# Five instead of two pairs of AC heads divided ahead of their flips, two heads on GpSimd, with all causal additions there

## The chip, the cores and the metric

One core of a Trainium2 chip runs the whole program in one launch. The metric is device time in microseconds (us), lower is better; of several runs the median counts. The profile is that of one execution.

## What is computed

Two layers of a decoder trunk on 256 tokens of width 1024, in float32. Each layer is half a SwiGLU feed-forward step, a mixer with three groups of heads, and a second half step:

```
h = h + 0.5 * swiglu(rms_norm(h, g1), w_gate1, w_up1, w_down1)
u = rms_norm(h, mix_norm);  P = u @ w_in
A: 4 query heads, one key/value head, keys chosen per query by an indexer (top 64)
B: 4 heads, plain causal attention (there is one block of 256 keys only)
C: 8 "forget" heads: s = q.k * scale + c[q] - c[k], c = cumsum(log_sigmoid(f + bias)),
   causal softmax, times v, times sigmoid(gate)
h = h + concat(o_A, o_B, o_C) @ w_out
h = h + 0.5 * swiglu(rms_norm(h, g2), w_gate2, w_up2, w_down2)
```

## The kernel before, in words

Every weight is split by ScalarE (L126, "high") and VectorE (L130, "low") into two float32r parts, and each product of the large matrices is three TensorE passes (`mm3`, L342). Weights come in by SyncE's DMA queue (L100) into five raw buffers; `Weights.pump`, `high` and `low` say where in the program order a unit is split. The schedule is manual: each engine runs its instructions in the order in which the program emits them, and waits where data or a buffer is not ready. TensorE's order, too, is the order of emission.

In a layer's mixer the loop at L1229 runs over the column chunks of `w_in` in 32 numbered steps (12 matmuls each for the chunks here); work on the side is hung on a step by `at_step(n, fn)` and run by `run_side`. Among it are the log gates and their running sums (`cumsum`, `sums_out`, `sums_in`, L902 to L922): a scan on VectorE, a write of the sums to DRAM, and three DMAs that read them back spread over all partitions into `first` (128 keys, all 8 heads; it takes over the buffer `tab`) and `later` (two tiles of 4 heads, `laterkT` and `laterlater`). The causal mask is added to the spread sums by `causal_part(i)` (L930): parts 0 and 1 on GpSimd at step 28, parts 2 and 3 on VectorE where the order below says `w2` and `w3`.

At step 30 the string EARLY is run, and after step 32 the string AC_ORDER. Each word is one piece of work, the letter what, the number a head or a pair of heads: `s` scores of a pair, `m` mask and row maximum of a head (L1092, VectorE), `e` its exponentials (L1102, ScalarE), `n` reciprocals of a pair's row sums (L1108), `d` a division of a head's probabilities (L1120; two instructions, of 128 and of 256 columns), `F`/`f` flips of a pair (24 TensorE transposes for its two heads, L180), `y` copies of the flipped pair out of PSUM (L193, one half of each bank on VectorE and ScalarE), `v` values, `o` the pair's output with its split (L1157), `h`/`r` parts of the output projection, `j`, `q`, `p` splits of weights. A- and C-heads are numbered 0 to 11, pairs 0 to 5; pairs 0 and 1 are the A-heads, 2 to 5 the forget heads.

Pairs in `divided` (0 and 1) have their probabilities divided before the flip. The others instead spread their reciprocals to 128x256 (`roots`, L1112), have that turned by four more transposes in the flip (L1131, `ident,tmp` in the profile), copied out with it (512 columns instead of 384), and for forget heads multiplied by the gate on GpSimd (L1144) before the output is multiplied by the result (L1165). `outT` then casts the output on ScalarE (L1172), and for forget heads takes the low part on GpSimd (L1180):

```
A.copy(hh, o)
oT[k] = (hh, hl)
high[p] = hl, o, hh, G if kind == "C" else V
if emit is None:
    low(p)
```

The B-heads run through the same functions at earlier steps, with the flip, the copies and the values in `both_scores` (L1204, the word `S`); their copies are all on ScalarE.

Of the kernel before, what the change touches and what calls it, by code (L numbers as in the profile page):

```python
# [10 lines left out]
F32 = mybir.dt.float32  # L11
# [3 lines left out]
ALU = mybir.AluOpType  # L15
# [3 lines left out]
P = 128  # L19
S = 256  # L20
D = 1024
# [5 lines left out]
TOPK = 64  # L27
# [10 lines left out]
WARM = 6  # L38
BRIDGE = 3
P_BUFS = 4  # L40
EARLY = "S Q q m0 e0 m1 e1 m2 e2 b0 b1 m3 j B0 B1 e3"
AC_ORDER = """
    h0 n0 d0 C n1 d1 d2 d3 T c0 F0 k0 F1 y0 y1 c1 k1 s2 v0 v1 m4 m5 g o0 o1 e4 e5 s3 s4
    h1 m6 m7 w2 e6 e7 l q q n2 n3 w3 m8 m9 h2 h3
    F2 f3 y2 y3 s5 v2 v3 e8 e9 m10 m11 e10 e11 o2 o3 n4 j
    r0 r1 n5 j F4 F5 y4 y5 h4 j v4 v5 o4 o5 j
    p h5 h6 h7 Z r2 N p r3 p r4 p M x2 p x3 p
"""
B_TURN, A_ROPE, B_STEP, A_ROOT, A_TURN, SUMS_STEP, TOP_STEP, A_STEP = 18, 18, 20, 21.3, 28.5, 21, 15, 30


CHUNKS = [
# [102 lines left out]
def kernel(ctx: ExitStack, tc: tile.TileContext, x, ffn1_norm, ffn1_w_gate, ffn1_w_up, ffn1_w_down,  # L155
# [10 lines left out]
    at = ctx.enter_context(tc.tile_pool(name="at", bufs=1))  # L166
# [5 lines left out]
    V, A, G, T = nc.vector, nc.scalar, nc.gpsimd, nc.tensor  # L172

    def bank(tag):
        return psum.tile([P, 512], F32, name="ps_" + tag, tag=tag)
# [6 lines left out]
    def turned(ps, dst, copies):  # L182
        for e, copy in enumerate(copies):
            d = dst[..., 64 * e:64 * e + 64]
            n = 64
            for k in d.shape[1:-1]:
                n *= k
            src = ps[e][:, :n]
            if len(d.shape) == 3:
                src = src.rearrange("p (b j) -> p b j", j=64)  # L190
            else:
                src = src.rearrange("p (a b j) -> p a b j", a=d.shape[1], j=64)
            copy(d, src)  # L193
# [4 lines left out]
    def tmp(n):  # L198
        return tp.tile([P, 512], F32, name="tmp", tag="tmp")[:, :n]
# [39 lines left out]
    W = Weights(tc, raw_pool, split_pool)  # L239
# [89 lines left out]
    causal = cp.tile([P, 3 * P], F32, name="causal")  # L329
# [12 lines left out]
    def mm3(o, lhs, rhs, start, stop):  # L342
        mm(o, lhs[0], rhs[0], start, False)
        mm(o, lhs[0], rhs[1], False, False)
        mm(o, lhs[1], rhs[0], False, stop)
# [344 lines left out]
    def mixer(l, norm, nxt):  # L690
        side, count = [], itertools.count()
        step = [0]

        def at_step(n, fn):
            side.append((n, next(count), fn))

        def run_side():
            due = sorted(x for x in side if x[0] <= step[0])
            for x in due:
                x[2]()  # L700
            side[:] = [x for x in side if x[0] > step[0]]
# [47 lines left out]
        st = {}  # L749
# [44 lines left out]
        def post_ib(ps):  # L794
# [10 lines left out]
            for t in range(2):  # L805
                x = small[t][:, None, 0:64]
# [24 lines left out]
                A.activation(la, la, AF.Ln, bias=1.0)  # L831
                A.activation(small[0][:, 0:1], ones[:, 0:1], AF.Exp)

            at_step(SUMS_STEP - 3, log_sigmoid)
            def forget():
                V.scalar_tensor_tensor(lf, fg, 0.0, la, op0=ALU.min, op1=ALU.subtract)

            at_step(SUMS_STEP - 2, forget)
            st["ikT"] = at.tile([P, 1, S], F32, name="ikT", tag="qs")

            def turn_ik():
# [42 lines left out]
                V.match_replace(out=st["score"][t], in_to_replace=m8, in_values=st["score"][t], imm_value=-3e38)  # L884

            def amask_begin():
                st["amask"] = at.tile([P, 3 * P], F32, name="amask", tag="amask")
                G.tensor_copy(st["amask"][:TOPK, 0:P], causal[:TOPK, 0:P])

            at_step(A_STEP - 4, amask_begin)  # L890

            def amask():
                am, score = st["amask"], st["score"]
                for d, x in ((am[:, P:], score[1]), (am[TOPK:, :P], score[0][TOPK:])):
                    V.tensor_scalar(d, x, -2e38, NEG, op0=ALU.is_gt, op1=ALU.mult)

            at_step(A_STEP - 0.5, amask)

            for r in range(TOPK // 8):
                at_step(TOP_STEP + 2 * r, lambda: topk(1))  # L900
# [20 lines left out]
                    nc.sync.dma_start(to, bass.AP(tensor=src.tensor, offset=src.offset + h * S,  # L921
                                                    ap=[[0, P], [S, k], [1, n]]))  # L922

            at_step(SUMS_STEP + 1, cumsum)
            at_step(SUMS_STEP + 3, sums_out)
            at_step(SUMS_STEP + 5, sums_in)
            for i in range(2):
                at_step(A_STEP - 2, lambda i=i: causal_part(i))

        def causal_part(i):  # L930
            x = st["first"][:, 2 * i:2 * i + 4] if i % 2 == 0 else st["later"][i // 2][:, :, 1]
            (V if i > 1 else G).tensor_tensor(x, x, causal[:, None, 0:P].to_broadcast([P, 4, P]), op=ALU.add)

        def post_a(ps):
            ss = sm.tile([P, 2, 5], F32, name="ssa", tag="ss")
# [40 lines left out]
        def post_b(ps):  # L976
# [34 lines left out]
            def qk_b(kind, h):  # L1011
                return st["bT"][:, h // 2 * 2], st["bT"][:, h // 2 * 2 + 1]

            st["B"] = run_heads([("B", h) for h in range(4)], qk_b, lambda i, fn: at_step(B_STEP + i, fn))

        c_ss = at.tile([P, 2, 2, 8], F32, name="c_ss", tag="c_ss")
# [35 lines left out]
        def tanh():  # L1052
            ps, hr = st.pop("cg"), st["hr"]
            sg = at.tile([P, 2, 512], F32, name="sg", tag="sg")
            for t in range(2):
                A.activation(sg[:, t], ps[t], AF.Tanh, scale=hr[:, t:t + 1])
            st["sg"] = sg
            for _ in range(2):
                bank("gu")


        def run_heads(hs, qk, emit=None):
            pj, pt, op, sums, bs, wide, flipped, gated, high = {}, {}, {}, {}, {}, {}, {}, {}, {}
            divided = range(2)
            blocks = ((slice(0, P), slice(0, P), slice(0, P)), (slice(P, 3 * P), slice(P, S), slice(0, S)))
            tag = "acc" if emit else "gu"

# [65 lines left out]
            def spread(p):  # L1133
                both = pp.tile([P, 8, P], F32, name="pT", tag="pT", bufs=2)
                kind, h = hs[2 * p]
                turned(flipped.pop(p), both[:, :6] if p in divided else both,
                       (A.copy if emit else V.tensor_copy, A.copy))
                pt[p] = [both[:, 3 * e:3 * e + 3].rearrange("p a b -> p (a b)") for e in range(2)]
                gated[p] = both[:, 6:8].rearrange("p a b -> p (a b)")
                if kind == "C":  # L1140
                    o = st["gate"][:, h // 2]
                    if p not in divided:
                        o = tmp(S)
                        G.tensor_tensor(o, gated[p], st["gate"][:, h // 2], op=ALU.mult)  # L1144
                    gated[p] = o
# [36 lines left out]
            if emit is None:  # L1182
                return scores, masks, exps, roots, divide, flip, spread, values, outT
# [10 lines left out]

        hs = [("A", h) for h in range(4)] + [("C", h) for h in range(8)]
        scores, masks, exps, roots, divide, flip, spread, values, outT = run_heads(hs, qk_ac)

        def c_T(ps, src, g, at):
# [5 lines left out]
        def both_scores(_):  # L1204
# [8 lines left out]
            for p in range(2):  # L1213
                b_values(p, st["keys"][p][:, S:])

        todo = dict(S=both_scores, D=divide, d=lambda i: divide(i, V), s=scores, m=masks, e=exps, n=roots, F=flip, y=spread, v=values, o=outT,
                    Q=lambda _: W.high(), q=lambda _: W.high(), j=lambda _: W.low(),
                    b=lambda p: st["B"][1](p), B=lambda p: st["B"][2](p), T=lambda _: tanh(), w=causal_part)

        def do(text):  # L1220
            for word in text.split():
                todo[word[0]](int(word[1:] or 0))

        at_step(A_STEP, lambda: do(EARLY))

        oT = {}
        posts = dict(ib=post_ib, a=post_a, b=post_b, ck=post_ck, cq=post_cq, cv=post_cv, cg=post_cg)
        index_queries()
        for name, cols in CHUNKS[1:]:  # L1229
            n = sum(c[1] for c in cols)  # L1230
            ps = [bank("gu") for _ in range(2)]
            for u in range(4):
                w = W.take()
                for kk in range(2):
                    k = 2 * u + kk
                    for t in range(2):
                        ts = slice(t * P, (t + 1) * P)
                        mm3(ps[t][:, :n], (norm.h[:, k, ts], norm.l[:, k, ts]), [v[:, kk] for v in w],
                            k == 0, k == KT - 1)
                step[0] += 1  # L1240
                run_side()
                if step[0] < A_STEP and step[0] != 8:
                    W.pump()
            posts[name](ps)
            if step[0] == 8:
                W.pump(2)
# [70 lines left out]
        def norm_out(_):  # L1317
# [5 lines left out]
            for t in range(2):  # L1323
# [3 lines left out]
                    p=lambda _: W.pump(), Z=residuals, N=norm_T, M=norm_out)  # L1327
# [23 lines left out]
    for l in range(DEPTH):  # L1351
        norm = ffn(norm, lambda: Norm(1, l), lambda: before_mixer(l), l == 0)
        norm = mixer(l, norm, lambda: Norm(2, l))
        norm = ffn(norm, (lambda: Norm(0, l + 1)) if l + 1 < DEPTH else None)
# [37 lines left out]
```

## Time and profile before

| | |
|---|---|
| median of 3 runs | 1001.65 us (1001.61 to 1001.83) |
| profiled execution, its own time | 1001.55 us |
| span of the profile, first to last instruction | 999.8 us |
| granted TensorE clock, mean | 0.999 |
| busy: PE, DVE, ACT, POOL | 995.5, 799.3, 597.4, 162.0 us |

Times in the timelines are microseconds from the start of the span. PE is TensorE's matmuls, PEld its weight loads, DVE VectorE, ACT ScalarE, POOL GpSimd, SPq SyncE's queue. The first layer's flips of forget heads lie between 294 and 302 us, the second layer's 494.9 us later, with the same instructions.

### The profile page before, as it was taken

What the parts mean: (1) busy time and instruction counts of PE and PEld (TensorE: products, weight loads), DVE (VectorE), ACT (ScalarE), POOL (GpSimd) and SP (SyncE); (2) the same over time, 40 slices, a digit from 0 to 9 for tenths busy, and PEclk for the clock granted to TensorE, in tenths of its full rate; (3) what the DMA queues carried; (4) which work ended last, traced back from release to release, by engine and by line L of the source; (5) the groups of instructions that cost most, each with busy time, mean ns of one, the idle gap of its engine ahead of it and who ended that gap; (6) DMA issues with size and microseconds to landing.
All of it is one profiled execution on the core that took longest, in us unless ns stands there. A gap on an engine that the chain in (4) does not pass through costs nothing.

```text
span 999.8 us, 15219 instructions
## 1 busy us (share of the span) xinstructions
PE 995.5 (100%) x5692; PEld 856.5 (86%) x5692; DVE 799.3 (80%) x1482; ACT 597.4 (60%) x1118; POOL 162.0 (16%) x188
## 2 busy tenths in 40 slices
PE   9999999999999999999999999999999999999998
PEld 8888888888878888888888888889888788888887
DVE  5978778789998777777888777787899977777775
ACT  6655555597786555555465555556968765555552
POOL 2003000058812000000000020001677210000000
PEclk9999999999999999999999999999999999999999
DMA  9865647475725555555655655565566164464731
GB/s 291 274 224 160 224 156 238 129 238 188 230 87 169 173 164 193 187 195 196 199 169 176 207 183 198 185 208 166 192 211 232 58 208 159 140 238 148 232 128 43
DMA packets 133498, 184.80 MB, mean 185 GB/s; under 512 B 7152, under 2 KB 106800, under 8 KB 133424
## 3 DMA queue, kind: packets, MB, share of 16 engines
q1 hardware_dynamic: 133392, 183.82, 56.2%
q8 instruction: 45, 0.74, 0.3%
q14 instruction: 29, 0.24, 0.1%
q10 hardware_dynamic: 32, 0.01, 0.0%
HBM read 182.75 MB, written 1.06 MB: 184 GB/s over the span
## 4 chain that ended last, share of the span: by engine, by line
PE 98%; DMA 1%; SPq 0%; ACT 0%; issue 0%; DVE 0%
PE ps_gu L340 66%; PE ps_acc L340 30%; PE ps_acc L180 1%; DMA raw<-in_ffn_w_up_dram 1%; PE ps_acc L375 1%; PE ps_gu L180 1%; SPq L100 0%; SPq L225 0%; PE ps_gu L375 0%; PE ps_acc L970 0%; ACT wh L126 0%; PE ps_acc L402 0%; PE ps_acc L844 0%; PE ps_acc L905 0%; DVE trunk L419 0%
## 5 line engine op out<-in xcount | busy, mean ns | idle before, releaser
L130 DVE TENSOR_TENSOR wl<-raw,wh 128x1024 fp32r<-128x1024 f32 (+2 forms) x342 | 421.6, 1240 | 27.1 <-ACT wh L126 27.1
L126 ACT CAST wh<-raw 128x1024 fp32r<-128x1024 f32 (+2 forms) x341 | 341.2, 1037 | 14.4 <-PE ps_acc L340 7.7
L340 PE MATMUL ps_gu<-xhl,wh 128*128 128x512 f32 (+1 forms) x1472 | 347.6, 388 | 0.2 <-ACT wh L126 0.2
L340 PEld LDWEIGHTS ps_gu<-xhl,wh 128*128 128x128 f32 x1472 | 272.5, 188 | 54.4 <-ACT wh L126 0.7
L340 PEld LDWEIGHTS ps_gu<-xhl,wl 128*128 128x128 f32 x1472 | 187.5, 191 | 4.1 <-DVE wl L521 0.2
L340 PE MATMUL ps_gu<-xhl,wl 128*128 128x256 f32 (+1 forms) x1472 | 190.3, 282 | 0.0
L484 DVE TENSOR_TENSOR tmp<-ps_gu,tmp 128x256 f32<-128x256 f32 x176 | 72.8, 422 | 109.3 <-ACT tmp L483 109.0
L340 PE MATMUL ps_acc<-wh,hh 128*128 128x512 f32 (+1 forms) x352 | 137.3, 390 | 0.0
L340 PE MATMUL ps_acc<-wl,hh 128*128 128x512 f32 (+1 forms) x352 | 137.0, 389 | 0.0
L340 PE MATMUL ps_acc<-wh,hl 128*128 128x512 f32 (+1 forms) x352 | 136.6, 388 | 0.0
L340 PE MATMUL ps_gu<-wh,xhl 128*128 128x512 f32 (+2 forms) x448 | 133.4, 375 | 0.0
L483 ACT COPY tmp<-ps_gu 128x256 f32<-128x256 f32 x176 | 63.4, 371 | 92.1 <-PE ps_gu L340 91.9
L498 ACT CAST hh<-tmp 128x256 fp32r<-128x256 f32 x80 | 32.6, 407 | 120.2 <-DVE tmp L495 120.2
L340 PEld LDWEIGHTS ps_gu<-wh,xhl 128*128 128x128 f32 x448 | 82.5, 188 | 14.1 <-issue 1.7
L490 ACT ACTIVATE tmp<-tmp 128x256 f32<-128x256 f32 x88 | 36.9, 419 | 82.7 <-DVE tmp L488 82.5
L340 PE MATMUL ps_gu<-wl,xhl 128*128 128x512 f32 (+2 forms) x224 | 83.2, 372 | 0.0
L351 POOL TENSOR_TENSOR y_n<-msq,minus_half 128x2 f32<-128x2 f32 x6 | 7.0, 1174 | 441.9 <-DVE msq L350 441.9
L340 PEld LDWEIGHTS ps_acc<-wh,hl 128*128 128x128 f32 x352 | 66.1, 188 | 13.9
L340 PEld LDWEIGHTS ps_acc<-wh,hh 128*128 128x128 f32 x352 | 66.2, 188 | 12.6
L340 PEld LDWEIGHTS ps_acc<-wl,hh 128*128 128x128 f32 x352 | 66.3, 188 | 12.3 <-DVE wl L130 0.2
L340 PEld LDWEIGHTS ps_gu<-wl,xhl 128*128 128x128 f32 x224 | 42.2, 188 | 5.9
L508 DVE TENSOR_TENSOR tmp<-tmp,rb 128x256 f32<-128x256 f32 x88 | 37.7, 428 | 3.0
(237 smaller groups left out, 901.5 us busy)
## 6 DMA issues: line engine op xcount, KB each, us to landing
raw<-in_ffn_w_down_dram SPq DMA_DIRECT2D x44, 1024.0 KB, 5.0
raw<-in_ffn_w_gate_dram SPq DMA_DIRECT2D x42, 1024.0 KB, 6.9
raw<-in_ffn_w_up_dram SPq DMA_DIRECT2D x42, 1024.0 KB, 7.8
raw<-in_w_in_dram SPq DMA_DIRECT2D x24, 1024.0 KB, 5.1
raw<-in_w_out_dram SPq DMA_DIRECT2D x8, 1024.0 KB, 5.0
raw<-in_w_in_dram SPq DMA_DIRECT2D x4, 768.0 KB, 5.0
raw<-in_w_in_dram SPq DMA_DIRECT2D x4, 656.0 KB, 4.2
raw<-in_ffn_w_gate_dram SPq DMA_DIRECT2D x3, 512.0 KB, 7.5
```

Of the source, the lines that this page charges most:

```text
L126: self.nc.scalar.copy(hv, src)
L130: (engine or self.nc.vector).tensor_tensor(lv, self.srcs[self.n_low], hv.bitcast(F32), op=ALU.subtract)
L180: T.transpose(b[:, 64 * i:64 * i + 64], src[r], ident[r, r])
L340: T.matmul(o, l, r, start=start, stop=stop, skip_group_check=True)
L351: G.tensor_tensor(y, dst, minus_half[:, :n], op=ALU.pow)
L375: T.transpose(ps[:, i, t * P:(t + 1) * P], trunk[:, t, (2 * mp + i) * P:(2 * mp + i + 1) * P], ident)
L483: A.copy(o, ps[:, 1])
L484: V.tensor_tensor(o, ps[:, 0], o, op=ALU.add)
L490: A.activation(th, t_, AF.Tanh, scale=0.5)
L498: (V.tensor_copy if late else A.copy)(hh, t_)
L508: V.tensor_tensor(t_, t_, norm.rb, op=ALU.mult)
```

## The change

It puts pairs 2, 3 and 4 into `divided`. Their heads are divided by VectorE (5, 6, 7, 9) and by GpSimd (4 and 8, the new word `G`). It moves the running sums (`cumsum` from step 22 to 26, `sums_out` from 24 to 27, `sums_in` from 26 to 28), the turn of the A-heads (28.5 to 26), the building of the A-mask and causal parts 0 and 1 (from steps 28 and 30 to the word `a` in EARLY), and one weight split (from step 29 to the word `j` in EARLY). Causal parts 2 and 3 go to GpSimd at the word `W`; all parts read a copy of the mask that VectorE (at `a`) and ScalarE (at `W`) write just before. One half of the B-heads' copies goes from ScalarE to VectorE.

```diff
-EARLY = "S Q q m0 e0 m1 e1 m2 e2 b0 b1 m3 j B0 B1 e3"
+EARLY = "S j a Q q m0 e0 m1 e1 m2 e2 b0 b1 m3 j B0 B1 e3"
 AC_ORDER = """
-    h0 n0 d0 C n1 d1 d2 d3 T c0 F0 k0 F1 y0 y1 c1 k1 s2 v0 v1 m4 m5 g o0 o1 e4 e5 s3 s4
-    h1 m6 m7 w2 e6 e7 l q q n2 n3 w3 m8 m9 h2 h3
-    F2 f3 y2 y3 s5 v2 v3 e8 e9 m10 m11 e10 e11 o2 o3 n4 j
-    r0 r1 n5 j F4 F5 y4 y5 h4 j v4 v5 o4 o5 j
+    h0 n0 d0 C n1 d1 d2 d3 T c0 F0 k0 F1 y0 y1 c1 k1 W s2 v0 v1 m4 m5 g o0 o1 e4 e5 s3 s4
+    h1 m6 m7 n2 G4 d5 e6 e7 l q q n3 d6 d7 m8 m9 h2 h3
+    F2 f3 y2 y3 s5 v2 v3 e8 e9 m10 m11 e10 e11 o2 n4 G8 d9 o3 j n5
+    r0 r1 j F4 F5 y4 y5 j h4 v4 v5 o4 o5 j
     p h5 h6 h7 Z r2 N p r3 p r4 p M x2 p x3 p
 """
-B_TURN, A_ROPE, B_STEP, A_ROOT, A_TURN, SUMS_STEP, TOP_STEP, A_STEP = 18, 18, 20, 21.3, 28.5, 21, 15, 30
+B_TURN, A_ROPE, B_STEP, A_ROOT, A_TURN, SUMS_STEP, TOP_STEP, A_STEP = 18, 18, 20, 21.3, 26, 26, 15, 30
...
-                st["amask"] = at.tile([P, 3 * P], F32, name="amask", tag="amask")
+                st["amask"] = at.tile([P, 4 * P], F32, name="amask", tag="amask")
...
-                for d, x in ((am[:, P:], score[1]), (am[TOPK:, :P], score[0][TOPK:])):
+                for d, x in ((am[:, P:3 * P], score[1]), (am[TOPK:, :P], score[0][TOPK:])):
                     V.tensor_scalar(d, x, -2e38, NEG, op0=ALU.is_gt, op1=ALU.mult)
-
-            at_step(A_STEP - 0.5, amask)
+                V.tensor_copy(am[:, 3 * P:], causal[:, 0:P])
+                for i in range(2):
+                    causal_part(i)
+
+            st["mask"] = amask
...
-            at_step(SUMS_STEP + 1, cumsum)
-            at_step(SUMS_STEP + 3, sums_out)
-            at_step(SUMS_STEP + 5, sums_in)
-            for i in range(2):
-                at_step(A_STEP - 2, lambda i=i: causal_part(i))
+            at_step(SUMS_STEP, cumsum)
+            at_step(SUMS_STEP + 1, sums_out)
+            at_step(SUMS_STEP + 2, sums_in)
...
-            (V if i > 1 else G).tensor_tensor(x, x, causal[:, None, 0:P].to_broadcast([P, 4, P]), op=ALU.add)
+            mask = st["amask"][:, None, 3 * P:].to_broadcast([P, 4, P])
+            G.tensor_tensor(x, x, mask, op=ALU.add)
+
+        def late_causal(_):
+            A.copy(st["amask"][:, 3 * P:], causal[:, 0:P])
+            for i in range(2, 4):
+                causal_part(i)
...
-            divided = range(2)
+            divided = range(5)
...
-                       (A.copy if emit else V.tensor_copy, A.copy))
+                       (V.tensor_copy, A.copy))
...
+G=lambda i: divide(i, G), W=late_causal, a=lambda _: st["mask"]()
...
-                if step[0] < A_STEP and step[0] != 8:
+                if step[0] < A_STEP - 1 and step[0] != 8:
                     W.pump()
+                if step[0] == A_STEP - 1:
+                    W.high()
```

The log gates stay at steps 18 and 19, written as plain numbers now.

## Rows read from the trace of the kernel before

**Rows 1.** The page, part 1: busy time, share of the span and instructions of each engine.

```profile
PE 995.5 (100%) x5692; PEld 856.5 (86%) x5692; DVE 799.3 (80%) x1482; ACT 597.4 (60%) x1118; POOL 162.0 (16%) x188
```

**Rows 2.** The page, part 4: the chain that ended last, shares by engine.

```profile
PE 98%; DMA 1%; SPq 0%; ACT 0%; issue 0%; DVE 0%
```

**Rows 3.** Waits of TensorE's weight loads, whole span: us in total, times, longest.

```profile
PEld ps_gu L340 <- issue: 3.7, 12, 0.4
...
PEld ps_acc L180 <- ACT pT L193: 0.4, 2, 0.2
```

**Rows 4.** Timeline, TensorE, layer 1: start, length, engine, line, tiles, count.

```profile
294.55 0.59 PE L180 MATMUL ps_gu<-ident,p 64*128 64x64 f32 x12
294.97 0.29 PE L180 MATMUL ps_gu<-ident,tmp 64*128 64x64 f32 x4
295.09 0.54 PE L180 MATMUL ps_acc<-ident,p 64*128 64x64 f32 x12
...
300.79 0.59 PE L180 MATMUL ps_gu<-ident,p 64*128 64x64 f32 x12
```

**Rows 5.** Timeline, ScalarE, layer 1: first exponential of head 8, cast of the outputs.

```profile
296.36 0.40 ACT L1102 ACTIVATE p<-tmp,nm 128x128 f32<-128x128 f32 x1
...
299.88 0.70 ACT L1172 CAST oh<-tmp 128x256 fp32r<-128x256 f32 x2
```

**Rows 6.** Timeline, ScalarE, layer 1: two copies of 384 and two of 512 columns.

```profile
285.32 0.86 ACT L193 COPY pT<-ps_gu 128x384 f32<-128x384 f32 x2
...
301.63 1.09 ACT L193 COPY pT<-ps_gu 128x512 f32<-128x512 f32 x2 [1.04 <-PE ps_gu L180]
```

**Rows 7.** Timeline, GpSimd, layer 1: gate products of pairs 2, 3, low parts.

```profile
296.12 1.42 POOL L1144 TENSOR_TENSOR tmp<-pT,cT 128x256 f32<-128x256 f32 x2 [20.03 <-ACT pT L193]
300.35 2.44 POOL L1180 TENSOR_TENSOR ol<-tmp,oh 128x256 fp32r<-128x256 f32 x2 [2.82 <-ACT oh L1172]
```

**Rows 8.** Timeline, VectorE, layer 1, around the flips of forget heads.

```profile
286.98 0.29 DVE L1092 CUSTOM_DVE_ANT_0 tmp<-ps_gu,tab 128x128 f32<-128x128 f32 x1
...
290.80 0.69 DVE L932 TENSOR_TENSOR tab<-tab,causal 128x512 f32<-128x512 f32 x1
...
295.29 0.69 DVE L193 COPY pT<-ps_gu 128x512 f32<-128x512 f32 x1 [0.67 <-PE ps_gu L180]
...
298.79 1.22 DVE L130 TENSOR_TENSOR wl<-raw,wh 128x1024 fp32r<-128x1024 f32 x1
...
300.43 1.75 DVE L130 TENSOR_TENSOR wl<-raw,wh 128x1024 fp32r<-128x1024 f32 x1
```

**Rows 9.** Timeline, GpSimd, layer 1: the division of one B-head.

```profile
263.51 0.60 POOL L1120 TENSOR_SCALAR p<-p,sums 128x128 f32<-128x128 f32 x1
...
264.09 0.92 POOL L1120 TENSOR_SCALAR p<-p,sums 128x256 f32<-128x256 f32 x1
```

**Rows 10.** Timeline, VectorE, layer 1: the divisions of heads 1 to 3.

```profile
283.53 1.44 DVE L1120 TENSOR_SCALAR p<-p,sums 128x128 f32<-128x128 f32 x6
```

**Rows 11.** Timeline, GpSimd and VectorE, layer 1: causal parts and the low beside them.

```profile
273.58 1.26 POOL L932 TENSOR_TENSOR tab<-tab,causal 128x512 f32<-128x512 f32 x1
274.81 1.27 POOL L932 TENSOR_TENSOR laterkT<-laterkT,causal 128x512 f32<-128x512 f32 x1
...
273.85 3.32 DVE L130 TENSOR_TENSOR wl<-raw,wh 128x1024 fp32r<-128x1024 f32 x1
```

**Rows 12.** Groups by line, whole span, VectorE: count, busy us, mean ns, idle before.

```profile
L1112 DVE COPY tmp<-sums 128x256 f32<-128x256 f32 x8 | 2.3, 294 | 0.3
```

**Rows 13.** Timeline, SyncE's queue, layer 1: issues of the sums and the weights.

```profile
258.83 0.41 SPq L911 DMA_DIRECT2D sums_of<-tmp  x1
...
263.60 0.37 SPq L921 DMA_DIRECT2D tab<-sums_of  x1
...
268.53 0.38 SPq L100 DMA_DIRECT2D raw<-in_ffn_w_gate_dram  x1
```

**Rows 14.** DMA issues, stretch 258 to 283 us: count, KB, us to landing.

```profile
laterkT<-sums_of SPq DMA_DIRECT2D x1, 512.0 KB, 7.5
```

More of the change, by code (lines that the diff above doesn't have):

```diff
@@ L832, in log_sigmoid @@
                 A.activation(small[0][:, 0:1], ones[:, 0:1], AF.Exp)
-            at_step(SUMS_STEP - 3, log_sigmoid)
+            at_step(18, log_sigmoid)
             def forget():
                 V.scalar_tensor_tensor(lf, fg, 0.0, la, op0=ALU.min, op1=ALU.subtract)
-            at_step(SUMS_STEP - 2, forget)
+            at_step(19, forget)
             st["ikT"] = at.tile([P, 1, S], F32, name="ikT", tag="qs")
@@ L1214, in both_scores @@
                 b_values(p, st["keys"][p][:, S:])
-        todo = dict(S=both_scores, D=divide, d=lambda i: divide(i, V), s=scores, m=masks, e=exps, n=roots, F=flip, y=spread, v=values, o=outT,
+        todo = dict(S=both_scores, D=divide, d=lambda i: divide(i, V), G=lambda i: divide(i, G), s=scores, m=masks, e=exps, n=roots, F=flip, y=spread, v=values, o=outT,
                     Q=lambda _: W.high(), q=lambda _: W.high(), j=lambda _: W.low(),
-                    b=lambda p: st["B"][1](p), B=lambda p: st["B"][2](p), T=lambda _: tanh(), w=causal_part)
+                    b=lambda p: st["B"][1](p), B=lambda p: st["B"][2](p), T=lambda _: tanh(), W=late_causal,
+                    a=lambda _: st["mask"]())
         def do(text):
```

## The prediction

> **What bounds the kernel now.** I read the page first: TensorE is busy for 995.5 us of a span of 999.8 [rows 1], and the chain of waits is 98% TensorE [rows 2]. A busy TensorE can hide short holes, so next come the waits of its weight loads: no single one is over 0.4 us outside the start, the largest sum (3.7 us in 12) waits for nothing the profile shows, and of the mixer's own waits the one that the change touches, for the copies of flipped B-heads, is 0.4 us in both layers together [rows 3]. So there are two ways to move the time: take instructions off TensorE, or make TensorE wait where it does not wait now. Work removed from VectorE, ScalarE or GpSimd is worth nothing by itself. So I laid the timelines of the four engines beside each other around the flips [rows 4, 5, 7, 8] and asked of each flip what it will wait for.
>
> The profiled execution took 1001.55 us, 1.75 more than its span and 0.1 under the median; I sum against 1001.55, and both layers of the mixer do the same, so each term counts twice. A difference under 0.2% (2.0 us) I call no change.
>
> **Taken off TensorE.** Three pairs lose the four transposes of their reciprocals. Four take 0.12 us, from the start of the `ident,tmp` group to that of the next [rows 4]: 0.37 us in a layer. This is certain and on the path: -0.37.
>
> **B-heads.** The copies out of PSUM are shared by two engines instead of four in a row on ScalarE. VectorE is free for them, because its weight split of that step moves behind them. That wait of TensorE is half of 0.4 us in a layer [rows 3]; I take all of it, -0.2, bounds -0.2 and 0.
>
> **Causal parts.** Now parts 0 and 1 stop VectorE: a split beside them took 3.32 us [rows 11], against 1.22 for one undisturbed [rows 8]. Moved to `a` they lie beside masks, which read one operand from PSUM; the gate products on GpSimd lie beside such masks too, and take 0.71 each [rows 7] as though alone. So nothing waits there, and VectorE reaches `m0` about 1 us earlier. It gains nothing from that: the word `C` writes a buffer that the last matmul of step 32 still reads, and after it VectorE divides heads 1 to 3 in 1.44 us [rows 10] just as now. Parts 2 and 3 leave VectorE (0.69 each [rows 8]), as do three spreads of reciprocals (0.29 each [rows 12]); the divisions that come in are shorter, 0.46 a head (a third of 1.44 [rows 10]), for four heads. VectorE waited 0.67 us for the flip of pair 2 [rows 8], so all this is slack exchanged for slack: 0.
>
> **Heads 4 and 5.** `G4` starts when `n2` is done, which now comes where part 2 stood, at 290.80 [rows 8]: about 291.0. It costs 0.60 + 0.92 = 1.52 us [rows 9]: 292.6 alone, and about 293.1 taking turns with heads 5 to 7 on VectorE. TensorE flips pair 2 at 294.55 [rows 4]. Hidden, with 1.5 us to spare: 0. For the division itself the row says 1.52 on GpSimd against 0.46 on VectorE [rows 9, 10]. The Trainium skill (GPSIMD Engine Reference, Performance versus the Vector engine) puts an elementwise instruction on GpSimd at 1.96 times VectorE's; by that the division would cost an estimated 0.9 us, and each hole below 0.6 us shorter: 1005.0 in place of the sum. The trace has the duration, so the sum goes by 1.52.
>
> **Head 8: the term that decides.** GpSimd runs in order, and the order is now `o2` (low part of pair 2's output), `G8`, low part of `o3`. The low part waits for the cast of the output on ScalarE, and that cast stands behind the exponentials of heads 8 to 11. In the trace GpSimd idles 2.82 us and starts the first low part at 300.35 [rows 7], because the cast starts only at 299.88 [rows 5]. Nobody minded: nothing was behind it but another low part. Now a division that TensorE's flip of pair 4 needs is behind it.
>
> - ScalarE: pair 2's flip ends 0.12 earlier without its four transposes, and its two copies have 384 instead of 512 columns, (1.09 - 0.86) / 2 = 0.12 each [rows 6]. So head 8's exponential starts at 296.36 - 0.36 = 296.0 [rows 5], the cast of `o2` 3.52 later (299.88 - 296.36, the same four heads) at 299.52, and the low part can start 0.47 after that (300.35 - 299.88) [rows 5, 7]: 300.0.
> - GpSimd: a low part takes 0.73 alone, and `G8` 1.52: the earliest end is 302.25.
> - VectorE's two splits at `j` fall into this. The first (1.22, about 298.9 to 300.05) delays nothing much. The second is ready at about 300.45, while the low part runs. In the trace the same pair met: a split of 1.75 instead of 1.22 us began at 300.43 [rows 8], 0.08 after the first low part, and two low parts together took 2.44 instead of 1.46 [rows 7]; they took turns, low part, split, low part. So I expect low part to 300.76, split to 301.9, `G8` to 303.4.
> - TensorE reaches this flip at 300.79 now [rows 4], and 0.25 earlier without the transposes of pairs 2 and 3: 300.54.
>
> The hole is 1.7 us if GpSimd goes first both times, 2.9 if the split goes between. I take 2.9, since the row with the same two instructions shows it. Behind the flip the copies, values and output parts of pairs 4 and 5 keep their distance from it, and GpSimd has one gate product less to do, so nothing more is lost and nothing is won back.
>
> The Trainium skill (SBUF — State Buffer, Who interferes with whom) says that the port shared by the two engines is locked for a whole instruction, for VectorE copies and tensor-scalar operations too. If divisions on VectorE are shut out in that way, heads 5 to 7 meet `G4` in its full length; by the rows that is a rival mechanism, priced as follows. VectorE's three divisions (1.4 us) and `G4` (1.52) one after the other end near 294.1, the masks of heads 8 and 9 near 295.2, and TensorE wants their banks at 295.34. That is a hole of 0 to 0.5 us in a layer, and it widens the range upward. No row shows a VectorE division beside a GpSimd instruction, so its chance, 0.15, is a guess that stands inside the forecast's.
>
> **Sums and DMAs.** The write of the sums now stands in SyncE's queue behind a 1 MB weight load issued at 268.53 [rows 13]. Now the reads are issued 4.8 us after the write [rows 13], so I expect them from 273.7; the second needs up to 7.5 us [rows 14], so part 1 can start between 279 and 281.6 and holds 1.26 us [rows 11]. The first forget mask is at 286.98 [rows 8]. Weight loads behind them land later, but what they bring is split only at the words `p`, after the last flip. Moving the A-heads' turn from one step to another leaves TensorE the same instructions: 0. The weight split moved into EARLY is the same instruction too; at worst it meets part 1 there and VectorE arrives at `C` as late as now.
>
> **Sum** for a layer: +2.9 - 0.37 - 0.2 = +2.3. Twice: +4.7, so 1001.55 + 4.7 = 1006.2. With the short hole and no split between: 2 x (1.7 - 0.57) = +2.3, 1003.8. With 0.5 more of `G4`: +5.7, 1007.2, and without the gain on the B-heads 1007.6.
>
> **Rivals.**
> - *No hole at head 8* (0.13). The flip finds head 8 ready. It would take `G8` ending before 300.5, so starting before 299.0, or the change not putting it behind the low part. For it: GpSimd is idle for 2.8 us just there [rows 7], and `n4` is done at about 298. Against it: both engines' orders are written out. Time: 1001.55 - 2 x 0.57 = 1000.4, no change.
> - *A second hole at heads 1 to 3* (0.10). The read of the sums lands later than 282, and the causal parts on GpSimd meet the divisions that TensorE's flip of pair 1 waits for with no slack. Two parts hold 1.26 each [rows 11], so 1.3 to 2.5 us more in a layer: 1008.8 to 1011.2. Against it: the loads that delay a read now would be through before it. It decides at 282.
> - *Faster* (0.04): holes that the busy row hides are larger than its waits say. All that is outside the busy time is 999.8 - 995.5 = 4.3 us [rows 1], most of it at the start and the ends; 2 us more than the 1.1 of certain gains would have to come from it: under 999.5.
>
> The forecast with its bounds has 0.73. With its own range (1003.8 to 1007.6) I take in the lower part of the second hole and an unknown or two below: 1002.8 to 1009.0. Slower is the forecast and the second hole, 0.83; no change 0.13; faster 0.04.
>
> **What would show it.** Right: in the changed kernel TensorE idles 1.5 to 3 us in each layer before the flip of pair 4, released by GpSimd's L1120; on GpSimd the low part of `o2` directly before that division, both after the cast at about 299.5 on ScalarE; the flips of pairs 2 to 4 with 12 transposes a bank and no `ident,tmp`; no idle time before the flip of pair 2. Wrong: TensorE's flip of pair 4 without a wait; a wait of over 0.5 us before the flips of pairs 1 or 2, or before forget scores; causal parts that last past 283; or a division on GpSimd that takes far less than 1.5 us.

## The result, and the profile after

The changed kernel takes **1011.1 us** (median of 5 runs, 1009.54 to 1012.42), against 1001.76 for the kernel before on the same chip (1001.61 to 1001.84): a ratio of 1.0092, 95% interval 1.008 to 1.0104. Slower was forecast, but at 1006.2 and in a range that ends at 1009.0. The profiled execution took 1010.73 us, with a span of 1009.0. One of the twelve runs of the last kernel below took 1410.2 us at a mean granted clock of 0.655, a slow run that is left out of that kernel's range and ratio.

Line numbers have moved: the division is L1127 (L1120 before), cast and low part of the outputs L1179 and L1187, masks L1099, spreads L1119, the scan L910, causal parts L934. First the page's engine row and the longest waits of TensorE's weight loads (us in total, times, longest), to be read against [rows 1] and [rows 3].

```profile
PE 998.7 (99%) x5668; PEld 858.8 (85%) x5668; DVE 798.7 (79%) x1494; ACT 595.5 (59%) x1116; POOL 170.0 (17%) x194
```

```profile
PEld ps_gu L180 <- POOL p L1127: 6.0, 4, 2.3
...
PEld ps_acc L340 <- DVE pT L193: 1.7, 2, 0.9
```

Two waits are new: 6.0 us for the division on GpSimd, which was forecast, and 1.7 us for the copies of the B-heads on VectorE, for which a gain was forecast. And TensorE is busy 3.2 us longer, although it has 24 transposes less. Three things are to be looked at.

**The hole before the flip of pair 4.** The timeline of the changed kernel, layer 1, of TensorE, VectorE, ScalarE and GpSimd:

```profile
301.12 0.39 PE L340 MATMUL ps_acc<-wh,ol 128*128 128x512 f32 x1
303.34 0.28 PE L180 MATMUL ps_gu<-ident,p 64*128 64x64 f32 x2 [1.83 <-POOL p L1127]
304.25 0.90 PE L180 MATMUL ps_gu<-ident,p 64*128 64x64 f32 x22 [0.63 <-POOL p L1127]
...
301.69 1.21 DVE L130 TENSOR_TENSOR wl<-raw,wh 128x1024 fp32r<-128x1024 f32 x1
...
300.41 0.70 ACT L1179 CAST oh<-tmp 128x256 fp32r<-128x256 f32 x2
...
300.88 0.73 POOL L1187 TENSOR_TENSOR ol<-tmp,oh 128x256 fp32r<-128x256 f32 x1 [7.29 <-ACT oh L1179]
301.60 2.60 POOL L1127 TENSOR_SCALAR p<-p,sums 128x128 f32<-128x128 f32 x2
304.16 0.72 POOL L1187 TENSOR_TENSOR ol<-tmp,oh 128x256 fp32r<-128x256 f32 x1
```

GpSimd idles 7.29 us until the cast is done, makes the low part, and only then divides head 8; VectorE's split of 301.69 falls into the first piece of the division, and the two pieces take 2.60 us instead of 1.52 [rows 9]. The split itself takes 1.21 us, as it does undisturbed, although the division started 0.09 us ahead of it. TensorE waits for the first piece (1.83) and again for the second (0.63). Against the same instructions of the kernel before it loses 1.9 and 0.8: 2.7 us, in layer 2 the same.

**The copies of the B-heads.** TensorE and VectorE of the changed kernel, layer 1, where the word `S` is:

```profile
275.66 0.70 PE L340 MATMUL ps_acc<-aT 64*128 64x128 f32 x5 [0.68 <-DVE pT L193]
...
267.22 0.66 DVE L910 TENSOR_TENSOR_SCAN tmp<-ones,ps_acc 8x256 f32<-8x256 f32 x1
...
269.77 1.93 DVE L130 TENSOR_TENSOR wl<-raw,wh 128x1024 fp32r<-128x1024 f32 x1
...
275.05 1.01 DVE L193 COPY pT<-ps_acc 128x384 f32<-128x384 f32 x2
```

The copies start at 275.05; before, VectorE stood at that place of its order at 273.85 [rows 11]. The 1.2 us come from the scan, which now runs here, and from a split of 1.93 instead of 1.22.

**TensorE's clock.** Stretches of the changed kernel (us of it, TensorE busy and matmuls, granted clock, DMA share, GB/s), behind the flips of layer 1 and of layer 2:

```profile
305.50:308.50 3.00, 3.00 (x23) 1.00 0.72 249
...
802.10:805.40 3.30, 3.00 (x29) 0.50 0.97 289
805.60:808.40 2.80, 2.80 (x14) 0.50 0.04 11
810.00:820.00 10.00, 10.00 (x50) 1.00 0.46 131
```

Behind the hole of layer 2 TensorE has 1.2 GHz instead of 2.4 for a while; behind the hole of layer 1, just as long, it keeps 2.4 GHz in this execution. The five runs differ in this: at a mean granted clock of 0.998 the kernel takes 1009.54 us, at 0.997 1010.73, at 0.996 1011.1 and 1011.15, at 0.995 1012.42. All runs of the kernel before stand at 0.999 or 1.0.

### The profile page after: what moved, and what is told of

It is laid out like the page before. It is cut to its first block, busy times and chain, and to the rows that moved or that the text cites. A ratio compares the mean times of both kernels' runs of the same rounds, so it can differ in the third digit from the quotient of the medians.

```text
span 1009.0 us, 15187 instructions
## 1 busy us (share of the span) xinstructions
PE 998.7 (99%) x5668; PEld 858.8 (85%) x5668; DVE 798.7 (79%) x1494; ACT 595.5 (59%) x1116; POOL 170.0 (17%) x194
## 3 DMA queue, kind: packets, MB, share of 16 engines
HBM read 182.75 MB, written 1.06 MB: 182 GB/s over the span
```

## The experiments

Eleven kernels, each timed in five rounds beside the kernel before (1001.74 us in the first group, 1001.65 in the others). All but the last two are the changed kernel with the edit shown.

### Head 8 on VectorE

```diff
-... e10 e11 o2 n4 G8 d9 o3 j n5
+... e10 e11 o2 n4 d8 d9 o3 j n5
```

> Theory: of the 9.3 us that the change costs, 5.5 are a hole of 2.74 in each layer before the flip of pair 4 (GpSimd holds head 8's division behind the low part of pair 2), about 3 are a stretch at half the granted clock that follows from that hole, 1.8 are late copies of the B-heads (0.9 a layer), and 0.7 is gained by 24 transposes less. With head 8 divided by VectorE the hole and the clock's fall go together: 1001.76 + 1.8 - 0.74 = 1002.8, granted clock 0.999, and no wait on line 1127 before that flip. Rival 1, the clock falls for another reason than the hole: 1011.1 - 5.5 = 1005.6 with a clock of 0.996 to 0.998. Rival 2, VectorE has no room for one more division (0.46) there either: a wait of 0.3 to 0.5 us before the flip remains, 1003.6.

1004.62 us (1003.88 to 1005.2), ratio 1.0028 [1.0018, 1.0038], granted clock 1.0 in all eight runs. No wait on L1127 is left. So 6.5 us of the 9.3 hang on head 8's division being on GpSimd there, and without it the clock does not fall. But the time is 1.8 us above the expectation: something else is late, which the hole had covered.

### Head 8 on GpSimd, ahead of the low part

```diff
-... e10 e11 o2 n4 G8 d9 o3 j n5
+... e10 e11 n4 G8 d9 o2 o3 j n5
```

> Theory: it is the place in GpSimd's order that makes the hole, not GpSimd's speed. With the division of head 8 ahead of the low part of pair 2 (nothing else changed on GpSimd) it starts when the reciprocal is there, near 298.3 us, ends before 300.5 even if a split on VectorE goes between its two pieces, and the flip does not wait: 1002.8 as with VectorE, clock 0.999. Rival: a division of 1.5 us and more on GpSimd is too long wherever it stands: a hole of 0.5 us or more remains in each layer, 1003.8 to 1005.5. Second rival: the low parts that now come 1.5 us later make the output projection wait, with the same time of 1004 or more, but with the wait at line 340.

1004.28 us (1003.92 to 1004.58), clock 0.999 to 1.0. TensorE and GpSimd of this run, layer 1:

```profile
301.29 0.96 PE L180 MATMUL ps_gu<-ident,p 64*128 64x64 f32 x24
...
298.98 1.58 POOL L1127 TENSOR_SCALAR p<-p,sums 128x128 f32<-128x128 f32 x2 [5.56 <-DVE sums L1115]
300.73 1.89 POOL L1187 TENSOR_TENSOR ol<-tmp,oh 128x256 fp32r<-128x256 f32 x2 [0.18 <-ACT oh L1179]
```

The weight loads of this run, whole span (us in total, times, longest):

```profile
PEld ps_acc L340 <- POOL ohl L1187: 0.8, 2, 0.4
```

The same division, as slow as before (1.58 us), costs nothing when it stands before the low part. The place in the queue is the cause, not the engine. But 1.5 us too much remain, as 1.8 did in the run before. The second rival's time came out, and there is a wait at line 340 as it said: 0.4 us in each layer for the low part of pair 4 on GpSimd (`ohl`). Its reason does not fit: the low part of pair 2 starts here as soon as the cast is done, and the run before, where no division stands ahead of it on GpSimd, shows the same line.

### B-copies on ScalarE, alone and with head 8 on VectorE

```diff
-                       (V.tensor_copy, A.copy))
+                       (A.copy if emit else V.tensor_copy, A.copy))
```

> Theory: the B-heads' copies cost 0.9 us a layer since VectorE reaches its half late. With all four on ScalarE as before, that part alone goes: 0.9 a layer, 1.8 to 2.0 in all, the hole at head 8 stays: 1009.1 if the clock stays as in the changed kernel (0.996), and the values of the B-heads start at most 0.2 us late. Rival: TensorE's delay at that place comes from elsewhere (the wait only shows on the copies because they are last), so that with the copies on ScalarE it waits as long: 1011. The spread of the runs should stay at 3 us, since the hole, and with it the fall of the clock, stays.

1009.29 us (1008.99 to 1009.61), 1.8 less than the changed kernel, at a clock of 0.996 to 0.997. The time is as expected: 0.9 us a layer is the price of the shared copies. The spread is not: these runs lie within 0.6 us, not 3, although the clock falls in all five.

> Theory: with both mended nothing is left of the change's cost, and the gain of the 24 transposes shows: 1001.76 - 0.74 = 1001.0, with a granted clock of 0.999 and runs within 0.5 us of one another. Rival: some of the cost lies in a part that no wait names (the moved sums, causal parts on GpSimd): 1001.8 or more. A fall to 1000.4 would say that the four copies on ScalarE wait no longer either.

1002.62 us (1002.22 to 1003.54), ratio 1.0008 [0.9999, 1.0016]. The two repairs add up (1004.62 - 2.0), but 1.6 us over the expected 1001.0 are left, as in the first two runs, and the runs differ by 1.3 us, not 0.5. The time is the rival's; that its causes (the moved sums, the causal parts) make it is not shown. TensorE and VectorE of this run, layer 1, behind the flip of pair 4:

```profile
304.01 1.52 PE L340 MATMUL ps_gu<-pT,va 128*64 128x256 f32 x16 [0.29 <-DVE pT L193]
...
298.52 1.01 DVE L1127 TENSOR_SCALAR p<-p,sums 128x128 f32<-128x128 f32 x4
...
299.78 1.21 DVE L130 TENSOR_TENSOR wl<-raw,wh 128x1024 fp32r<-128x1024 f32 x1
...
301.65 1.75 DVE L130 TENSOR_TENSOR wl<-raw,wh 128x1024 fp32r<-128x1024 f32 x1
303.32 1.14 DVE L193 COPY pT<-ps_gu 128x384 f32<-128x384 f32 x2
```

The first split started at 298.79 and the second at 300.43 before [rows 8]; now both are 1.0 to 1.2 us later, after the divisions (1.01), and the copies behind them let the values wait. With the wait for `ohl`, which this run shows too (0.8, 2, 0.4), that is 0.3 and 0.4 us in each layer, about the 0.8 that is left; the kernel before has neither wait.

### The scan back at step 22

Head 8 is on VectorE, the B-copies are shared.

```diff
-            at_step(SUMS_STEP, cumsum)
+            at_step(22, cumsum)
```

> Head 8 is divided by VectorE here, so the comparison is with that run (1004.62). Theory: the copies of the B-heads come late (a wait of 0.9 us in each layer, 1.7 to 2.0 in all) because the scan of the log gates was moved from step 22, where VectorE had room, to step 26, just ahead of them, and a split there then fell beside a GpSimd instruction (1.93 instead of 1.22 us). With the scan back at step 22 and nothing else changed, VectorE's copies start about 1.2 us earlier and the wait on line 193 goes: 1002.7. Rival: the split meets GpSimd with or without the scan; then only the scan's 0.5 us comes back and some 0.4 us of wait remain in each layer: 1003.6. Second rival: the copies on VectorE are late because of the split that stands ahead of them alone: no change, 1004.6.

1002.22 us (1001.95 to 1003.03), 2.4 less than without the edit: a little more than the wait itself. VectorE and TensorE of this run, layer 1:

```profile
269.53 1.22 DVE L130 TENSOR_TENSOR wl<-raw,wh 128x1024 fp32r<-128x1024 f32 x1
...
274.10 1.01 DVE L193 COPY pT<-ps_acc 128x384 f32<-128x384 f32 x2
...
274.88 0.82 PE L340 MATMUL ps_acc<-aT 64*128 64x128 f32 x8
```

The copies are 0.95 us earlier, the split is at 1.22 again, and TensorE waits for neither. Gone too is the 0.4 us for these copies that the kernel before has [rows 3]: against all four on ScalarE (1002.62) this is 0.4 less, the gain that the prediction gave the shared copies. The rival (the split meets GpSimd anyway) falls. The order of the two had changed: in the changed kernel GpSimd's product (L720) started at 269.58, 0.19 before the split, and here the split starts ahead of it:

```profile
269.58 3.03 POOL L720 TENSOR_TENSOR cqa<-cqa,y_cq 128x512 f32<-128x512 f32 x2
```

```profile
269.90 3.74 POOL L720 TENSOR_TENSOR cqa<-cqa,y_cq 128x512 f32<-128x512 f32 x2
```

(The first fence is the changed kernel, the second this run.) In this pair the second pays: VectorE 0.7 us, or GpSimd's two products 0.7. It is no rule of these traces: in the hole of the changed kernel the division was first, by 0.09 us, and paid.

### The split moved behind the copies

Head 8 is on VectorE, the B-copies are on ScalarE.

```diff
-    r0 r1 j F4 F5 y4 y5 j h4 v4 v5 o4 o5 j
+    r0 r1 F4 F5 y4 y5 j j h4 v4 v5 o4 o5 j
```

> Compared with the run that has head 8 on VectorE and the B-copies on ScalarE (1002.62), which was 1.6 above the sum without any hole. Theory: those 0.8 us a layer are VectorE, which is 1.2 us late after the two divisions of heads 8 and 9 (1.0 us) and so reaches its copies of pairs 4 and 5 late, behind a split of 1.75 us: TensorE's values wait 0.3 us and what follows 0.4 more. With that split moved behind the copies, its next users at the output projection still in time, the copies start 1.6 us earlier: 1002.62 - 1.4 = 1001.2. Rival: the loss comes from the low parts on GpSimd or from ScalarE's casts; then at most 0.3 us comes back, 1002.3. Third: the moved split now delays the output projection, 1003 or more.

1003.59 us (1003.48 to 1004.28), 1.0 **more**: a miss, at the third rival's time. TensorE and VectorE and GpSimd of this run, layer 1:

```profile
303.47 1.52 PE L340 MATMUL ps_gu<-pT,va 128*64 128x256 f32 x16
...
307.92 0.73 PE L340 MATMUL ps_acc<-wh,ohl 128*128 128x512 f32 x2 [0.83 <-POOL ohl L1187]
...
306.07 1.21 DVE L130 TENSOR_TENSOR wl<-raw,wh 128x1024 fp32r<-128x1024 f32 x1
...
306.38 2.18 POOL L1187 TENSOR_TENSOR ohl<-tmp,ohl 128x256 fp32r<-128x256 f32 x2 [1.98 <-ACT ohl L1179]
```

The first half of the theory held: the copies come in time, and the values start 0.54 us earlier without a wait. But now the low part of pair 4 on GpSimd begins 0.3 us after a split and stands behind it (2.18 for two low parts, 1.46 alone), and TensorE waits 0.83 for it, in layer 2 the same. It is this low part that delays the output projection, not the moved split itself, as the third rival had it. One late VectorE was exchanged for another wait of the same kind.

### The hole in one layer only

```diff
-G=lambda i: divide(i, G)
+G=lambda i: divide(i, G if i == 4 or l == 0 else V)
```

(For layer 2, `l == 1`.)

> Only in layer 1 does GpSimd divide head 8; in layer 2 VectorE does. Theory: the granted clock falls as a consequence of the hole, in whichever layer it is. Then this lies half way between 1004.62 (no hole) and 1011.1 (two holes): 1007.9, the clock at half its speed only in a stretch right behind the flip of pair 4 of layer 1, mean 0.998. Rival: the fall has another cause, in layer 2 or over the whole run: then here it is 1004.62 + 2.0 to 2.7 = 1006.6 to 1007.3 with a clock of 0.999 to 1.0, or the stretch at half the clock lies in layer 2.

> The mirror: GpSimd divides head 8 in layer 2 only. Theory: 1007.9 again, the stretch at half the clock behind the flip of pair 4 of layer 2, none in layer 1. Rival (the fall belongs to layer 2 or to the length of the run): 3.4 us from the clock all in this run and none in its mirror, so 1009.5 to 1010 here and 1006.6 there.

1007.84 us (1006.34 to 1009.36) and 1008.1 us (1006.68 to 1009.26): half way, both. The stretches behind the flips of layer 1 and layer 2, first with the hole in layer 1 only, then in layer 2 only:

```profile
305.50:308.50 3.00, 3.00 (x19) 0.50 0.91 314
...
802.10:805.40 3.30, 3.00 (x37) 1.00 0.01 2
```

```profile
305.50:308.50 3.00, 3.00 (x23) 1.00 0.92 290
...
802.10:805.40 3.30, 3.30 (x10) 0.50 0.68 236
```

The clock falls where the hole is and nowhere else, so it is a consequence of the hole. In each of the two kernels one run of five kept a mean clock of 1.0, at 1006.34 and 1006.68; against 1004.62 that is the hole's own net price, 1.7 and 2.1 us, and the rest up to the median, 1.5 and 1.4 us, is the clock's. That net price is below the 2.7 us of the hole, because the hole also hides the about 0.8 us a layer that 1004.62 still holds (1.5 to 1.8 in both layers).

### The hole without the split in it

```diff
-    r0 r1 j F4 F5 y4 y5 j h4 v4 v5 o4 o5 j
+    r0 r1 F4 F5 y4 y5 j j h4 v4 v5 o4 o5 j
```

> The changed kernel with head 8 still behind the low part on GpSimd, but VectorE's second split moved behind its copies of pairs 4 and 5, so that it can't go between the low part and the division. Theory: of the hole of 2.74 us about 1.1 is that split; the first piece of the division then takes 0.6 to 0.7 instead of 1.69 us and TensorE waits 1.6 to 1.7 us in each layer, the other value that the prediction gave. The move by itself cost 1.0 us in both layers together where there was no hole: 1011.1 - 2.2 + 0 to 1.0 = 1008.9 to 1009.9. The clock still falls behind the hole, perhaps for less. Rival: the split only fills time that GpSimd waits anyway, for the reciprocal or for the first split: the hole stays at 2.7 and the time at 1011 to 1012.

1009.25 us (1008.37 to 1009.4), in the expected band. TensorE, then GpSimd of this run, layer 1:

```profile
302.30 0.28 PE L180 MATMUL ps_gu<-ident,p 64*128 64x64 f32 x2 [0.78 <-POOL p L1127]
303.20 0.90 PE L180 MATMUL ps_gu<-ident,p 64*128 64x64 f32 x22 [0.62 <-POOL p L1127]
...
304.16 0.68 PE L340 MATMUL ps_acc<-wh,oh 128*128 128x512 f32 x1
304.63 0.63 PE L340 MATMUL ps_acc<-wl,oh 128*128 128x512 f32 x1
305.06 0.63 PE L340 MATMUL ps_acc<-wh,ol 128*128 128x512 f32 x1
...
301.60 1.54 POOL L1127 TENSOR_SCALAR p<-p,sums 128x128 f32<-128x128 f32 x2
```

The division takes 1.54 us again, so the split was worth 1.06 us of the hole. The wait that is left, 0.78 and 0.62, is still followed by matmuls at 0.43 us from start to start, against 0.23 at the full clock: four runs of five show a mean of 0.997 or 0.998.

### Pairs 2 and 3 only

Pair 4 keeps its spread reciprocal, and the order around it is the old one; first with the B-copies on ScalarE, then with shared copies and the scan at step 22.

```diff
-            divided = range(5)
+            divided = range(4)
...
-... e10 e11 o2 n4 G8 d9 o3 j n5
-    r0 r1 j F4 ...
+... e10 e11 o2 o3 n4 j
+    r0 r1 n5 j F4 ...
```

> Pair 4 goes back to a spread reciprocal and the words around it to their old order; pairs 2 and 3 stay divided (head 4 on GpSimd), the B-copies are all on ScalarE. Theory: hole, late copies of pairs 4 and 5, and the fall of the clock all hang on pair 4; pairs 2 and 3 are free on every engine. Then only the gain of 16 transposes is left: 1001.65 - 0.5 = 1001.15, and no wait of over 0.5 us in the mixer. Rival: the moved sums, the causal parts on GpSimd or the division of head 4 there cost something that the larger losses covered: 1001.7 or more.

1001.84 us (1001.49 to 1002.21), ratio 1.0003 [0.9994, 1.0011]: no gain, the rival's number. In layer 1 of its profile TensorE waits for the low part of pair 4, which began 0.29 us after a split of VectorE:

```profile
307.44 0.74 PE L340 MATMUL ps_acc<-wh,ohl 128*128 128x512 f32 x2 [0.34 <-POOL ohl L1187]
...
305.57 1.22 DVE L130 TENSOR_TENSOR wl<-raw,wh 128x1024 fp32r<-128x1024 f32 x1
...
305.86 2.21 POOL L1187 TENSOR_TENSOR ohl<-tmp,ohl 128x256 fp32r<-128x256 f32 x2 [0.66 <-ACT ohl L1179]
```

> The same with the B-copies shared by VectorE and ScalarE, and the scan back at step 22. Theory: the copies no longer come late, and the wait of 0.4 us for them in both layers together, which the kernel before has, goes too, as the prediction had it for the change: 1000.9, 0.75 under the kernel before. Rival: VectorE is no faster there than four copies in a row on ScalarE, and it is as the run with ScalarE's copies, 1001.15.

**1000.72 us** (1000.35 to 1000.92), ratio 0.999 [0.9981, 0.9999], 0.9 under the kernel before and 10 under the changed one: it beats both, the first narrowly, by less than the 2.0 us below which the prediction speaks of no change. TensorE is busy 994.7 us, and no wait of the mixer is longer than 0.4 us; here the low part of pair 4 started at 305.36, before the split of 305.42:

```profile
PE 994.7 (100%) x5676; PEld 856.3 (86%) x5676; DVE 798.5 (80%) x1492; ACT 595.8 (60%) x1116; POOL 167.4 (17%) x192
```

```profile
305.42 1.77 DVE L130 TENSOR_TENSOR wl<-raw,wh 128x1024 fp32r<-128x1024 f32 x1
...
305.36 2.43 POOL L1187 TENSOR_TENSOR ohl<-tmp,ohl 128x256 fp32r<-128x256 f32 x2 [0.32 <-ACT ohl L1179]
```

Against the run with the scan back and pair 4 divided on VectorE (1002.22) this is 1.5 less, with eight more transposes and the old order of the words around pair 4: its division is not worth its place on VectorE.

## Why the prediction was right and wrong

**Right: the direction, and the term that decides.** The hole is at the flip of pair 4, released by the division, behind the low part of `o2` and the cast on ScalarE. It was put at 2.9 us in a layer and is 2.7. The details were other than forecast: the split fell into the division's first piece, not ahead of it; TensorE started on the first piece and waited again for the second; and all of it came 0.9 us later, by the late copies. The size agrees because the split's 1.1 us lengthen the hole at either place; the value without the split was put at 1.7, and without the split TensorE's two waits are 1.06 shorter (0.78 + 0.62 against 1.83 + 0.63). The 24 transposes are gone at the rate forecast: the flips of pairs 2 and 3 each gain 0.12.

**Wrong: "B-heads".** The step said that VectorE is free for the copies and took -0.2 a layer. It looked only at what stands behind the copies in VectorE's order, and took VectorE's arrival from the kernel before. But the same change had put the scan (0.66 us) ahead of it, and the prediction's "sums" step had looked only at the DMAs of the sums, not at the scan on VectorE. Late by 1.2 us, the copies cost +0.9; with the scan back the kernel took 2.4 us less, 1.2 a layer. For both layers -0.4 was forecast and +1.8 to +2.0 measured: 2.2 to 2.4 of the 4.9 us that the forecast of 1006.2 missed.

**Wrong: the clock is not in the sum.** The sum priced a hole by its length, and so put the clock at nothing without saying so. Behind a hole TensorE can run at 1.2 GHz for a while; by the one-layer runs that is 1.4 to 1.5 us in the median for each, 2.9 for both.

With these two the sum closes: 1001.76 - 0.74 + 2 x 2.7 + 2 x 0.9 + 2.9 = 1011.1. It closes for the median; a single execution can differ, as the profiled one, whose clock fell behind one hole only.

**Covered, and wrong without the cover: "slack exchanged for slack: 0".** That step counted VectorE's divisions and found them hidden. For heads 5 to 7 that held: the flip of pair 2 waits for nothing. For head 9 (and 8, where VectorE makes it) it did not: VectorE comes 1.0 to 1.2 us late to two splits and the copies behind them, about 0.8 us a layer. In the changed kernel the hole hides it, so it took no part in the miss. The last kernel shows that the 1.5 us too much of the repaired kernels hang on pair 4's division; that they are these late copies and the late low part is read from the traces, since the one repair tried made another wait.

**Heads 4 and 5** were hidden as forecast; the division on GpSimd took 1.57 us, beside two pieces on VectorE of 0.66:

```profile
292.03 1.57 POOL L1127 TENSOR_SCALAR p<-p,sums 128x128 f32<-128x128 f32 x2 [1.42 <-DVE sums L1115]
...
291.89 0.66 DVE L1127 TENSOR_SCALAR p<-p,sums 128x128 f32<-128x128 f32 x2
```

Two pieces on VectorE alone took 0.55 in the run without the split in the hole. So the rival mechanism of a port locked against divisions for a whole instruction, with its 0 to 0.5 us, did not show in this meeting, in which VectorE was first by 0.14 us. The Trainium skill (SBUF — State Buffer, Who interferes with whom) has that lock for VectorE instructions with two SBUF inputs, and for copies and tensor-scalar operations whose operands meet its conditions; the rows here agree for VectorE's splits, which read two operands from SBUF and are delayed by GpSimd's instructions (1.93 instead of 1.22 us) or delay them (2.60 instead of 1.52), but for divisions they show 0.1 us. The Trainium skill (GPSIMD Engine Reference, Performance versus the Vector engine) gives 1.96 times VectorE's time for an elementwise addition on GpSimd; the division here is 1.57 against 0.55 us, 2.9 times.

**Rivals.** "No hole" fell. "A second hole at heads 1 to 3" fell too, although the time that it gave (1008.8 to 1011.2) came out: the second causal part started at 281.47 and took 1.44, so it lasted to 282.9, before its mark of 283, and no wait is there. "Faster" fell. The causal parts 2 and 3 beside the masks slowed neither.

## What to carry to other kernels

When a change puts work into an engine's queue, look at what stands ahead of it there and what that waits for: a slow engine was harmless before the low part and cost 6.5 us behind it. When several things move at once, first make the new timeline of each engine up to every point where TensorE needs it, and only then judge a step; a scan moved for one reason made copies late that were moved for another. And price a hole like these in TensorE above its length, since its clock can fall behind it; whether it does is seen in the granted clock of the stretches behind it and in the mean of each run.

## What the runs showed of the hardware that was not expected

TensorE's granted clock halves behind waits as short as 0.78 and 0.62 us within one flip, and not in every run: four of five with these waits show a lower mean, and so do four of five with a hole in one layer only, with waits of the length of 1.83 and 0.63. That makes a hole worth 0 to 3 us more than it lasts (1006.34 to 1009.36 for one kernel), and lets the runs of a kernel differ by up to 3 us, where those without a hole differ by 1.3 at most; but it need not, since the kernel with both holes and the B-copies on ScalarE differs by 0.6. A single wait of 0.83 us in each layer, with the split behind the copies, left the mean at 1.0 in all eleven runs. What separates the two kinds of wait was not tried.

VectorE's splits and GpSimd's instructions take turns, and a shift of a few tenths of a microsecond decides which of them pays: the same pair cost VectorE 0.7 us or GpSimd 0.7, and one low part that began 0.29 us after a split made TensorE wait in one run where, 0.06 before the split, it did not in the other.
